# Three engines in program order in the neighbourhood attention, bias as one row of keys, weight splits last in a step

## The chip, the cores and the metric

The kernel runs on one core of a Trainium2 chip. Its engines work in parallel, each through its own list of instructions: TensorE (PE; its weight loads are PEld), VectorE (DVE), ScalarE (ACT), GpSimd (POOL), and SyncE (SP), which issues most DMAs. An instruction that needs another engine's result waits on a semaphore. The metric is the time of one execution on the device in microseconds (us).

## The reference, cut to what matters

The layer computes one input projection, two groups of attention heads, and an output projection with a residual. The change touches the second group, neighbourhood attention: 16 heads of width 64 on a grid of 16 rows x 64 columns, where each token attends to a window of 8 x 16 tokens and to 16 meta tokens.

```python
q = _rmsnorm(q, q_w); k = _rmsnorm(k, k_w)          # per head
# per grid row r: keys of 8 rows, per column a window of 16 columns
bias = rel_bias[:, dr_idx[None, :, None], dc_idx[:, None, :]]
s_win = einsum('bqhd,brqchd->bhqrc', q_row, k_win) * scale + bias
s_meta = einsum('bqhd,bmhd->bhqm', q_row, k_meta) * scale + meta_b
p = softmax(concatenate([s_win, s_meta], axis=-1), axis=-1)
o = einsum('bhqrc,brqchd->bqhd', p_win, v_win) + einsum('bhqm,bmhd->bqhd', p_meta, v_meta)
y_na = o * silu(g_na)
```

The input width is 1024, there are 1024 tokens, all in float32.

## The kernel before

Three phases follow one another. The first (to about 198 us) normalizes the input, transposes it to `hT`, and computes all gates; in its gaps it builds the relative bias (`base`, L381) and lays it out per head pair (`stage_bias`, GpSimd, written to `bias_d`). The second, which the change is about, is the neighbourhood attention, to about 735 us. Latent attention and the output projection follow.

Products in float32 are made of two halves of fewer bits: `wnh`/`wnl` of a weight, `hT`/`hTl` of the input, `qz`/`qs` of a query, two halves of keys in `kM`, of the softmax in `PT`, of values in `Vt`. The high half is a copy on ScalarE (or the other named engine), the low half a subtraction, mostly on VectorE (`lo_of`, L106), which therefore always waits for the copy.

The neighbourhood attention takes 8 head pairs of 8 tiles of 128 tokens. The loop (L691 on) runs over steps `g`. Each does a piece for four tiles at different stages: the 24 projection matmuls of the tile six ahead (`proj`, into `ps_acc`), in three parts; pv of the tile one behind (`na_pv`, `ps_o`); the transposes of the softmax of tile `g`, head 0 and head 1 (`na_ptr`, giving PT0 and PT1); the scores of the next tile (`na_qk`: TensorE into `ps_s`, VectorE adds the bias and takes the minimum into `s_sb` and `nmn`, ScalarE takes exp and its sum); the transposes of a normalized q and k (`na_tr`: on ScalarE two kM copies and two qz, then on VectorE two kM and two qs). `na_acc` takes the projection out of its bank (squares `sqn`, copy `raw`, `Vt`), every second time with the norm (`rstd`: ssn, constants, pow on GpSimd, a step of refinement). Tile 1 of a pair also projects the meta keys (16 matmuls onto `hM`). Tiles 2 to 5 load and split a quarter of the next pair's weights each. The last six steps project the latent instead (`lat_nat`).

The banks of scores and transposes are one pool of four (`bank("s")`, `bank("tr")`).

TensorE's instructions are in the order of the code. Those of ScalarE, VectorE, GpSimd and SP are ordered by the framework's scheduler when the kernel is built, by its own estimate of when each can run; on the chip every engine then follows its list.

Of the kernel before, what the change touches and what calls it, by code (L numbers as in the profile page):

```python
# [18 lines left out]
P = 128  # L19
# [15 lines left out]
WB = WI + 2 * WE  # L35
# [14 lines left out]
def hybrid_layer(ctx, tc, x, x_t, meta, meta_t, norm_w, w_na, w_g, w_lat, lat_w, w_uq, w_ukv, vec128, qpe_w, kpe_w,  # L50
# [27 lines left out]
    bias_d = dram.tile([NPAIR, P, 2, WB], F32, name="bias_d")  # L78
# [4 lines left out]

    def rstd(ss, n, cnt, np_=P, E=G):
# [3 lines left out]
        t = small.tile([P, n], F32, name="rs_t", tag=f"rs_t{n}")[:np_]  # L88
# [6 lines left out]
        G.tensor_tensor(y, v, mhalf[:np_, :n], op=ALU.pow)  # L95
        E.tensor_tensor(t, y, y, op=ALU.mult)
# [6 lines left out]
        return y  # L103

# [238 lines left out]
    base = sp1.tile([P, 16, NB, ROWS], F32, name="base")  # L343
# [33 lines left out]
    def bias_rows(rk):  # L377
        ps = bank("tr" if rk % 2 else "o")[:, :384].rearrange("p (h b) -> p h b", h=16)
        mm(ps, selr[:, rk, :], rbh, True, False)
        mm(ps, selr[:, rk, :], rbl, False, True)  # L380
        V.tensor_scalar(base[:, :, :, rk], ps, -1.0, rmask[:, rk:rk + 1], op0=ALU.mult, op1=ALU.add)  # L381


    sg = sctx.enter_context(tc.tile_pool(name="stg", bufs=1))

    imask = load(c_imask, [P, WI], "imask", sp1)
    metab = load_bc(meta_bias, 16 * NM, "metab", sp1).rearrange("p (h m) -> p h m", h=16)
    G.tensor_scalar(metab, metab, -1.0, None, op0=ALU.mult)

    def stage_bias(p):  # L390

        E = G
        bs = base[:, 2 * p:2 * p + 2].rearrange("p h b r -> p h (b r)")
        bo = sg.tile([P, 2, WB], F32, name="sgb", bufs=3)
        bi, b0, b7 = bo[:, :, :WI], bo[:, :, WI:WI + WE], bo[:, :, WI + WE:]
        mb = metab[:, 2 * p:2 * p + 2, :]
        im = imask[:, None, :].to_broadcast([P, 2, WI])
        for o, bb, w in ((0, 0, 128), (144, 8, 128), (288, 16, 112)):
            E.tensor_tensor(bi[:, :, o:o + w], bs[:, :, bb * 16:bb * 16 + w], im[:, :, o:o + w], op=ALU.add)
        E.memset(bi[:, :, 128:144], MASK)  # L400
        E.tensor_copy(bi[:, :, 272:288], mb)
        for b_, c in ((b0, 128), (b7, 0)):
            E.tensor_copy(b_[:, :, 0:128], bs[:, :, c:c + 128])
            E.tensor_copy(b_[:, :, 128:144], mb)
            E.tensor_copy(b_[:, :, 144:272], bs[:, :, c + 128:c + 256])
        G.dma_start(bias_d[p], bo)

    todo_b = list(range(NPAIR))
# [12 lines left out]
    sctx.close()  # L421
# [45 lines left out]
    def na_nat(src, n, width):  # L467

        sq = np2.tile([P, 512], F32, name="sqn")[:n, :width]
        raw = np2.tile([P, P], F32, name="natm", bufs=1)[:n, :width]  # L470
        S.activation(sq, src, AF.Square)
        S.copy(raw, src)
        return na_norm(sq, raw, n, width)

    def na_norm(sq, raw, n, width):
# [3 lines left out]
        r = rstd(ss, g, 1.0 / 64, n, V)  # L479
        r3 = raw.rearrange("p (g d) -> p g d", g=g)  # L480
        V.tensor_tensor(r3, r3, r[:, :, None].to_broadcast([n, g, 64]), op=ALU.mult)
        return raw
# [17 lines left out]
    def na_meta(p):  # L500
        d = st[p]
        acc = bank("s")
        proj(acc[:, :256], NT, d["w"], 128, 384)
        kv = np2.tile([P, 256], F32, name="kvm", bufs=1)[:NM]
        meta_sum(kv, acc[:, :256])
        Vm = VM[p % 2]
        v_split(Vm, kv[:, 128:256], NM)
        d["Vm"] = Vm
        d["natm"] = na_nat(kv[:, :128], NM, 128)
# [7 lines left out]
    def na_acc(p, t, acc):  # L517
# [43 lines left out]
    def na_qk(p, t):  # L561
# [7 lines left out]
        for j in range(2):  # L569
# [59 lines left out]
    def na_sum(p, hf):  # L629
# [9 lines left out]
               r.rearrange("p t j -> p (t j)")[:, :, None].to_broadcast([P, 8, 64]))  # L639
        ps = bank("tr")  # L640
# [20 lines left out]
    def lat_nat(t, acc, q, sq, pieces=None):  # L661
# [570 lines left out]
def _tables():  # L1232
# [30 lines left out]
    im[:, 0:128] = cm[:, 0:128]  # L1263
    im[:, 144:272] = cm[:, 128:256]
# [50 lines left out]
```

## Time and profile before

| | |
|---|---|
| median of 3 runs | 1379.38 us (1378.87 to 1380.16) |
| profiled execution | 1379.65 us, of which the span 1377.8 us |
| mean granted clock of TensorE | 0.985 |
| busy, share of the span | PE 96%, PEld 88%, DVE 70%, ACT 59%, POOL 32% |
| the chain that ended last | PE 69%, DVE 15%, ACT 4%, DMA 3% |

The profile is of one execution. A busy time is the time in which the engine ran an instruction; a timeline row gives in square brackets how long the engine had been idle before and which instruction's end let it go on. A row of groups gives after the bar the busy time, the mean length of one, and the idle time ahead of the group with its releasers.

### The profile page before, as it was taken

Reading aid. Unit: us, or ns where it says so; the run is one execution under the profiler, and the core shown is the slowest. Engines: PE = TensorE matmul, PEld = TensorE weight load, DVE = VectorE, ACT = ScalarE, POOL = GpSimd, SP = SyncE. Lnnn points to the kernel's source line nnn. Section 1 sums busy time; section 2 is a strip of 40 time slices with the busy share of each in tenths; the row PEclk is TensorE's granted clock in tenths of the full one; section 3 lists DMA queues with packets and bytes.
Section 4 is the critical chain, followed back from the end, with each engine's and each line's share of the span. In section 5 each row is a group of like instructions: output and inputs, shape, how many; then the busy total and the mean of one; then the engine's idle time right before and its main releaser. Section 6 shows DMA issues by size and latency. Waiting matters only on the chain.

```text
span 1377.8 us, 24771 instructions
## 1 busy us (share of the span) xinstructions
PE 1316.7 (96%) x8116; PEld 1214.6 (88%) x8116; DVE 958.1 (70%) x3101; ACT 809.8 (59%) x2271; POOL 436.4 (32%) x936
## 2 busy tenths in 40 slices
PE   8989998999899999999889889999999999999998
PEld 7868888998898989889889889999999999988887
DVE  4924335887877888788768998987987988642110
ACT  6522124776767777777756667777777777630110
POOL 5330472121111211132344545734734652000000
PEclk9999999999999999999999999999999999999999
DMA  9352373222322222221111100100010022254231
GB/s 342 109 175 94 125 284 91 62 78 67 98 59 78 60 74 67 74 71 55 51 43 36 55 31 21 36 28 25 27 33 29 29 77 72 83 168 130 71 109 46
DMA packets 85694, 112.24 MB, mean 81 GB/s; under 512 B 10679, under 2 KB 63287, under 8 KB 85447
## 3 DMA queue, kind: packets, MB, share of 16 engines
q1 hardware_dynamic: 84415, 102.94, 24.1%
q0 software_dynamic: 1152, 7.73, 1.4%
q8 instruction: 64, 1.05, 0.3%
q14 instruction: 63, 0.52, 0.1%
HBM read 75.12 MB, written 29.23 MB: 76 GB/s over the span
## 4 chain that ended last, share of the span: by engine, by line
PE 69%; DVE 15%; ACT 4%; DMA 3%; issue 2%; POOL 1%; SPq 0%; DVEq 0%; ACTq 0%; POOLq 0%
PE ps_acc L109 21%; PE mps_acc L109 10%; PE ps_s L109 8%; PE mps_s L109 7%; PE mps_st L109 6%; PE mps_o L109 5%; PE ps_tr L112 4%; PE mps_tr L112 4%; PE ps_o L109 4%; DVE u_na L626 2%; DVE m_sb L988 1%; DVE PT L106 1%; DVE mPT L106 1%; ACT m_sb L997 1%; DMA Vp<-Vt 1%
## 5 line engine op out<-in xcount | busy, mean ns | idle before, releaser
L95 POOL TENSOR_TENSOR rs_y<-rs_v,mhalf 128x1 f32<-128x1 f32 (+5 forms) x170 | 148.2, 875 | 139.4 <-DVE rs_v L91 115.4
L109 PE MATMUL ps_acc<-wnh,hT 128*128 128x384 f32 (+1 forms) x432 | 163.3, 378 | 6.0 <-DVE Vt L106 4.5
L109 PE MATMUL ps_acc<-wnl,hT 128*128 128x384 f32 (+1 forms) x432 | 147.2, 341 | 0.0
L109 PE MATMUL ps_acc<-wnh,hTl 128*128 128x384 f32 (+1 forms) x432 | 147.1, 340 | 0.0
L547 POOL CAST qs<-qz 64x128 fp32r<-64x128 f32 x128 | 42.1, 329 | 298.3 <-ACT qz L543 281.2
L109 PE MATMUL mps_s<-mkT,mq 128*128 128x346 f32 (+1 forms) x576 | 132.1, 338 | 1.4 <-DVE mPT L106 1.0
L578 ACT ACTIVATE s_sb<-s_sb,nmn 128x400 f32<-128x400 f32 (+1 forms) x128 | 76.9, 601 | 61.2 <-DVE nmn L576 47.8
L109 PE MATMUL mps_o<-mPT,mV 128*128 128x256 f32 x768 | 106.2, 287 | 0.0
L1014 ACT CAST mPT<-mps_tr 128x512 fp32r<-128x512 f32 x128 | 74.4, 583 | 51.1 <-PE mps_tr L112 50.2
L988 DVE TENSOR_SCALAR_CACHE_REDUCE m_sb<-mps_s 128x346 f32<-128x346 f32 (+1 forms) x192 | 97.1, 512 | 9.0 <-PE mps_s L109 7.1
L106 DVE TENSOR_TENSOR mPT<-mps_tr,mPT 128x512 fp32r<-128x512 f32 x128 | 87.6, 685 | 13.3 <-ACT mPT L1014 12.1
L109 PEld LDWEIGHTS mps_s<-mkT,mq 128*128 128x128 f32 x576 | 93.3, 192 | 3.2 <-DVE mPT L106 1.6
L109 PEld LDWEIGHTS mps_o<-mPT,mV 128*128 128x128 f32 x768 | 94.9, 189 | 0.2
L109 PEld LDWEIGHTS ps_acc<-wnh,hT 128*128 128x128 f32 x432 | 84.7, 196 | 7.4 <-DVE Vt L106 4.8
L997 ACT ACTIVATE m_sb<-m_sb,mnm 128x1040 f32<-128x1040 f32 x64 | 74.6, 1166 | 23.2 <-DVE mnm L996 16.4
L109 PEld LDWEIGHTS ps_acc<-wnl,hT 128*128 128x128 f32 x432 | 84.6, 196 | 0.0
L109 PEld LDWEIGHTS ps_acc<-wnh,hTl 128*128 128x128 f32 x432 | 83.5, 193 | 0.0
L106 DVE TENSOR_TENSOR PT<-ps_tr,PT 128x384 fp32r<-128x384 f32 (+2 forms) x160 | 72.1, 467 | 12.7 <-ACT PT L599 11.8
L599 ACT CAST PT<-ps_tr 128x384 fp32r<-128x384 f32 (+2 forms) x160 | 62.0, 411 | 28.7 <-PE ps_tr L112 27.8
L112 PE MATMUL mps_tr<-ident,m_sb 128*128 128x128 f32 x512 | 76.7, 273 | 2.0 <-DVE mq L106 1.0
L109 PE MATMUL ps_o<-PT,Vt 128*128 128x256 f32 x256 | 60.5, 299 | 15.7 <-DVE PT L106 15.6
L106 DVE TENSOR_TENSOR kM<-ps_tr,kM 64x128 fp32r<-64x128 f32 x144 | 41.6, 289 | 34.8 <-ACT qz L543 30.1
(483 smaller groups left out, 3977.7 us busy)
## 6 DMA issues: line engine op xcount, KB each, us to landing
wnf<-in_w_na_dram SPq DMA_DIRECT2D x32, 384.0 KB, 3.3
g_d<-g SPq DMA_DIRECT2D x32, 256.0 KB, 2.7
wnf<-in_w_out_dram SPq DMA_DIRECT2D x32, 256.0 KB, 2.7
bias_d<-sgb POOLq DMA_DIRECT2D x8, 944.0 KB, 4.5
wnf<-in_w_g_dram SPq DMA_DIRECT2D x19, 384.0 KB, 6.5
Vp<-Vt SPq DMA_DIRECT2D x48, 112.0 KB, 2.2
yfo<-y_d SPq DMA_DIRECT2D x24, 192.0 KB, 2.8
b<-bias_d SPq DMA_DIRECT2D x16, 272.0 KB, 3.4
```

Of the source, the lines that this page charges most:

```text
L95: G.tensor_tensor(y, v, mhalf[:np_, :n], op=ALU.pow)
L106: eng.tensor_tensor(dst, src, f(hi), op=ALU.subtract)
L109: T.matmul(o, lhsT=l, rhs=r, start=start, stop=stop, skip_group_check=True)
L112: T.transpose(out=o, in_=i, identity=ident[: i.shape[0], : i.shape[0]])
L547: G.tensor_copy(qs[h_, j], qz[l_, j])
L578: S.activation(sb, sb, AF.Exp, scale=-1.0, bias=mn, accum_out=d["sum", t // 4][:, t % 4, j:j + 1])
L599: S.copy(pt[:n, c0:c1, 0, :], ps[:n, c0:c1])
L626: V.tensor_tensor(u[a], u[a], o[a], op=ALU.add)
L988: V.tensor_scalar(st["sb", h, t][:, ks], s_ps, -SCALE, BIG, op0=ALU.mult, op1=ALU.min, accum_out=st["mx", h, t][:, b:b + 1])
L997: S.activation(sb, sb, AF.Exp, scale=-1.0, bias=nm, accum_out=st["ms", h, t // 2][:, t % 2:t % 2 + 1])
L1014: S.copy(dh, ps)
```

## The change

For the whole loop of the neighbourhood attention, the change puts ScalarE, VectorE and GpSimd under `manual_schedule`: their lists follow the code. The code of a step is rearranged. The exps of both heads come after both minima. The second half of `rstd` and the scaling (`na_acc2`) come one odd step later. The meta keys are taken out of their bank in four pieces over tiles 1, 2 and 3. The weights' splits are the last but one thing of a step. `na_sum` is in two halves. The latent tile is scaled at the beginning of the next step (`late`). The weights of the latent projection are split over tiles 2 to 4 and 7 of the last pair.

The bias is one row of 416 keys: `base` is built with its gaps for the meta keys in place, written by one DMA, and read once per pair; VectorE adds the mask of an interior tile (`bi`, 128x800) once per pair. The copies of GpSimd are gone, and the low halves of the last two groups of gate weights move from VectorE to GpSimd. The first pair's weights are loaded and split before the last gates.

```diff
-WB = WI + 2 * WE
+WB = 416
...
+    def rstd2(vy, n, np_=P, E=G):
+
+        v, y = vy
+        t = small.tile([P, n], F32, name="rs_t", tag=f"rs_t{n}")[:np_]
...
+    basek = base.rearrange("p h (g c) -> p h g c", c=144)
...
+        V.tensor_scalar(basek[:, :, :, rk:128:16], ps.rearrange("p h (g b) -> p h g b", g=3), -1.0, rmask[:, rk:rk + 1],
+                        op0=ALU.mult, op1=ALU.add)
...
+    for k in range(2):
+        V.tensor_scalar(basek[:, :, k, 128:], metab, -1.0, None, op0=ALU.mult)
...
-        gw = g_load(gr, (G, G) if gr < 4 else (V, V))
+        gw = g_load(gr)
+        if gr == 5:
+            for k in range(4):
+                na_load(0, k)
...
-                elif gr > 3 and todo_b:
-                    stage_bias(todo_b.pop(0))
-    sctx.close()
+        if gr == 3:
+            nc.sync.dma_start(bias_d.rearrange("h p n -> p h n"), base[:, :, :WB])
+            sctx.close()
...
+    imask = load(c_imask, [P, WI], "imask", np1)
+
+    def na_bias_load(p):
+        bs = st[p]["bs"] = np2.tile([P, 2, WB], F32, name="bs")
+        nc.sync.dma_start(bs, bias_d[2 * p:2 * p + 2].rearrange("h p n -> p h n"))
+        st[p].update(b0=bs[:, :, 144:], b7=bs[:, :, :WE])
 
     def na_bias(p):
-        c = 0
-        for name, w, n in (("bi", WI, 2), ("b0", WE, 1), ("b7", WE, 1)):
-            t = st[p][name] = np2.tile([P, 2, w], F32, name=name, bufs=n)
-            nc.sync.dma_start(t, bias_d[p, :, :, c:c + w])
-            c += w
+
+        bi = st[p]["bi"] = np2.tile([P, 2, WI], F32, name="bi", bufs=1)
+        V.tensor_tensor(bi, st[p]["bs"][:, :, :WI], imask[:, None, :].to_broadcast([P, 2, WI]), op=ALU.add)
...
+        if t % 2:
+            d["vy"] = na_norm1(sq, P, 512), raw
+
+    def na_acc2(p, t):
+        d = st[p]
+        vy, raw = d["vy"]
+        na_norm2(vy, raw, P, 512)
+        d["nat"][t - 1], d["nat"][t] = raw[:, :256], raw[:, 256:]
...
+            d["p", t, j] = sb, mn
+        for j in range(2):
+            sb, mn = d["p", t, j]
             S.activation(sb, sb, AF.Exp, scale=-1.0, bias=mn, accum_out=d["sum", t // 4][:, t % 4, j:j + 1])
-            d["p", t, j] = sb
...
+    def lat_nat2(t, acc, nat, r):
+        V.tensor_scalar(nat[:, :256], acc[:, :256], r[:, 0:1], None, op0=ALU.mult)
+        V.tensor_scalar(nat[:, 256:], acc[:, 256:], r[:, 1:2], None, op0=ALU.mult)
+        nats["pe", t] = nat[:, 256:]
...
+        if late is not None:
+            late.append(lambda: lat_nat2(t, acc, nat, r))
+            return
...
+    mctx = ExitStack()
+    mctx.enter_context(tc.manual_schedule(engines={mybir.EngineType.Activation, mybir.EngineType.DVE,
+                                                   mybir.EngineType.Pool}))
...
-            if 1 < t < 6 and p + 1 < NPAIR:
-                na_load(p + 1, t - 2)
-            if t == 2 and p + 1 == NPAIR:
-                wk = w_load(lambda k: w_lat[:, 2 * k:2 * k + 2, 256:576], 320, (G, V))
...
+        if late:
+            late.pop()()
+        if on(pr) and t == 2:
+            na_meta2(p)
+        if on(b - 1) and (b - 1) % 4 == 3:
+            na_sum((b - 1) // NT, (b - 1) % NT // 4)
         if on(b):
             na_pv(*divmod(b, NT))
+        if on(pr - 2) and pr % 2:
+            na_acc2(*divmod(pr - 2, NT))
...
+            na_acc(p, t, acc)
             if t == 1:
                 na_meta(p)
-            na_acc(p, t, acc)
+            if t == 2:
+                na_meta3(p)
             if t == 3:
+                na_meta4(p)
                 na_meta_tr(p)
-            if t == 7 and p + 1 < NPAIR:
-                na_bias(p + 1)
+            if 1 < t < 6:
+                k = t - 2
+                if p + 1 < NPAIR:
+                    na_load(p + 1, k)
+                    if k == 3:
+                        na_bias_load(p + 1)
+                elif k < 3:
+                    wk.append(w_split(w_lat[:, 2 * k:2 * k + 2, 256:576], 320, (V, V)))
+            if pr == NSTEP - 1:
+                wk.append(w_split(w_lat[:, 6:8, 256:576], 320, (V, V)))
         elif a < NSTEP:
-            lat_nat(t, acc, False, np2.tile([P, 512], F32, name="sqn")[:, :256])
+            lat_nat(lt, acc, False, np2.tile([P, 512], F32, name="sqn")[:, :256], late=late)
...
+        if a % NT == 7 and on(a + 1):
+            na_bias((a + 1) // NT)
         if on(b - 1) and (b - 1) % 4 == 3:
-            na_sum((b - 1) // NT, (b - 1) % NT // 4)
+            na_sum2((b - 1) // NT, (b - 1) % NT // 4)
```

On ScalarE, an interior step of the middle of the phase, before (`PT_1738` and `PT_1740` are PT0 and PT1, `qz` the queries' high half):

```order
L578 ACTIVATE s_sb,nsum<-s_sb,nmn 128x400
L599 CAST PT_1738<-ps_tr 128x3x128
L638 COPY rx<-nr 128x512
L578 ACTIVATE s_sb,nsum<-s_sb,nmn 128x400
L599 CAST PT_1740<-ps_tr 128x3x128
L578 ACTIVATE s_sb,nsum<-s_sb,nmn 128x400
L524 ACTIVATE sqn<-ps_acc 128x256
L525 COPY raw<-ps_acc 128x256
L464 CAST Vt<-ps_acc 128x2x64
L489 CAST kM<-ps_tr 64x128 x2
L543 ACTIVATE qz_1729<-ps_tr,qkw_na 64x128 x2
```

and the same engine now (`PT_1662` and `PT_1664`):

```order
L612 CAST PT_1662<-ps_tr 128x3x128
L592 ACTIVATE s_sb,nsum<-s_sb,nmn 128x400 x2
L612 CAST PT_1664<-ps_tr 128x3x128
L481 CAST kM<-ps_tr 64x128 x2
L554 ACTIVATE qz_1653<-ps_tr,qkw_na 64x128 x2
L530 ACTIVATE sqn<-ps_acc 128x256
L531 COPY raw<-ps_acc 128x256
L460 CAST Vt<-ps_acc 128x2x64
L497 COPY kvm<-ps_s 16x256
```

PT1's copy stood ahead of the second exp of its own step, and now stands behind both; the kM copies and qz follow it directly, ahead of `sqn`, `raw` and `Vt`.

On VectorE a step with a weight split, before (`ISA s_sb` is the minimum with the bias, `PT_1738` and `PT_1740` as above):

```order
L106 TENSOR_TENSOR Vt<-ps_acc,Vt 128x128
L106 TENSOR_TENSOR PT_1738<-ps_tr,PT_1738 128x3x128
L106 TENSOR_TENSOR wnl<-wnf,wnh 128x384 x2
L576 ISA s_sb,nmn<-ps_s,bi 128x400
L576 ISA nmn 128x1
L106 TENSOR_TENSOR wnl<-wnf,wnh 128x384
L576 ISA s_sb,nmn<-ps_s,bi 128x400
L576 ISA nmn 128x1
L106 TENSOR_TENSOR wnl<-wnf,wnh 128x384
L106 TENSOR_TENSOR PT_1740<-ps_tr,PT_1740 128x3x128
L478 TENSOR_REDUCE ssn<-sqn 128x8
L106 TENSOR_TENSOR Vt<-ps_acc,Vt 128x128
```

and a step now (`PT_1661` is PT0, `PT_1663` PT1):

```order
L639 TENSOR_TENSOR u_na<-u_na,ps_o 64x512 x2
L640 TENSOR_TENSOR y_na<-u_na 128x256
L114 TENSOR_TENSOR PT_1661<-ps_tr,PT_1661 128x3x128
L587 ISA s_sb,nmn<-ps_s,bi 128x400
L587 ISA nmn 128x1
L587 ISA s_sb,nmn<-ps_s,bi 128x400
L587 ISA nmn 128x1
L114 TENSOR_TENSOR PT_1663<-ps_tr,PT_1663 128x3x128
L114 TENSOR_TENSOR kM<-ps_tr,kM 64x128 x2
L557 SCALAR_TENSOR_TENSOR qs<-ps_tr,qkw_na,qz_1652 64x128 x2
L114 TENSOR_TENSOR Vt<-ps_acc,Vt 128x128
```

The low halves of weights stood between the minima and PT1; now PT1 follows the second minimum directly, kM, qs and Vt follow PT1, and the weights follow these.

On SP, at the end of the gates, before (`wnf` are weights of the pairs, `g_d` a gate's result, `naw` the norm's weights):

```order
L258 DMA g_d<-g_1584 128x512
L143 DMA wnf<-in_w_na_dram 128x768
L258 DMA g_d<-g_1655 128x512
L143 DMA wnf<-in_w_na_dram 128x768 x2
L258 DMA g_d<-g_1698 128x512
L143 DMA wnf<-in_w_na_dram 128x768 x2
L69 DMA naw<-in_na_w_dram 128x2
L458 DMA bi<-bias_d 128x2x400
```

and now:

```order
L151 DMA wnf<-in_w_na_dram 128x768 x3
L266 DMA g_d<-g_1517 128x512
L151 DMA wnf<-in_w_na_dram 128x768
L266 DMA g_d<-g_1607 128x512
L266 DMA g_d<-g_1637 128x512
L69 DMA naw<-in_na_w_dram 128x2
L69 DMA imask<-in_c_imask_dram 128x400
L566 DMA Vp<-Vt 112x256
L565 DMA Vp<-Vm_1657 16x256 x2
L151 DMA wnf<-in_w_na_dram 128x768
```

Two loads of weights that stood ahead of `naw` are behind it now.

## Rows read from the trace of the kernel before

**Rows 1.** Stretches by engine: us, busy time and (instructions) of each, PEclk (1.00 full), DMA
```profile
150.00:197.70 47.70, 47.70 (x210) 39.08 (x209) 16.80 (x27) 9.91 (x20) 37.97 (x93) 1.00 0.62 220
317.25:563.20 245.95, 231.79 (x1445) 221.27 (x1445) 202.06 (x609) 180.67 (x536) 50.21 (x84) 0.97 0.25 72
```

**Rows 2.** Timeline from 450.5 us: start, us, engine, line, operation, out<-in, count [idle before]
```profile
450.94 0.35 PE L109 MATMUL ps_s<-kM,qz 128*128 128x400 f32 x1
...
452.59 0.57 DVE L576 CUSTOM_DVE_ANT_0 s_sb<-ps_s,bi 128x400 f32<-128x400 f32 x1
...
453.15 0.56 DVE L576 CUSTOM_DVE_ANT_0 s_sb<-ps_s,bi 128x400 f32<-128x400 f32 x1
...
453.88 0.62 ACT L578 ACTIVATE s_sb<-s_sb,nmn 128x400 f32<-128x400 f32 x1
...
457.46 0.34 PE L109 MATMUL ps_s<-kM,qz 128*128 128x400 f32 x1
```

**Rows 3.** Timeline from 443 us, all engines
```profile
444.89 0.56 DVE L106 TENSOR_TENSOR PT<-ps_tr,PT 128x384 fp32r<-128x384 f32 x1 [0.72 <-ACT PT L599]
...
445.82 0.36 PE L109 MATMUL ps_s<-wnh,hM 128*48 128x256 f32 x1
...
446.57 0.54 ACT L489 CAST kM<-ps_tr 64x128 fp32r<-64x128 f32 x2
...
447.14 0.75 ACT L543 ACTIVATE qz<-ps_tr,qkw_na 64x128 fp32r<-64x128 f32 x2
...
447.78 0.34 PE L109 MATMUL ps_acc<-wnh,hT 128*128 128x384 f32 x1
...
447.92 0.61 DVE L106 TENSOR_TENSOR kM<-ps_tr,kM 64x128 fp32r<-64x128 f32 x2 [0.66 <-ACT qz L543]
```

**Rows 4.** TensorE's waits, 232.9 to 673.9 us: total, times, longest
```profile
PE ps_o L109 <- DVE PT L106: 14.1, 12, 2.1
```

**Rows 5.** Timeline of TensorE from 498.5 us
```profile
499.08 0.39 PE L109 MATMUL ps_o<-PT,Vt 128*128 128x256 f32 x1 [2.10 <-DVE PT L106]
...
503.06 0.52 PE L109 MATMUL ps_acc<-wnh,hTl 128*128 128x384 f32 x1
503.38 0.38 PE L109 MATMUL ps_acc<-wnh,hT 128*128 128x384 f32 x1
```

**Rows 6.** VectorE's groups, four periods: busy us, mean ns | idle before, releasers
```profile
L106 DVE TENSOR_TENSOR PT<-ps_tr,PT 128x384 fp32r<-128x384 f32 x48 | 26.4, 550 | 5.8 <-ACT PT L599 5.5
...
L106 DVE TENSOR_TENSOR kM<-ps_tr,kM 64x128 fp32r<-64x128 f32 x72 | 20.8, 289 | 16.0 <-ACT qz L543 13.4 <-PE ps_acc L109 1.3
...
L478 DVE TENSOR_REDUCE ssn<-sqn 128x8 f32<-128x512 f32 x16 | 11.0, 686 | 11.1 <-ACT sqn L524 11.1
```

**Rows 7.** ScalarE's groups in the same stretch
```profile
L599 ACT CAST PT<-ps_tr 128x384 fp32r<-128x384 f32 x48 | 22.9, 476 | 13.5 <-PE ps_tr L112 13.2
```

**Rows 8.** GpSimd's groups, 150 to 198 us
```profile
L399 POOL TENSOR_TENSOR sgb<-base,imask 128x256 f32<-128x256 f32 (+1 forms) x24 | 17.5, 754 | 52.4 <-DVE base L381 51.6 <-DMA bias_d<-sgb 0.7
```

**Rows 9.** Chain of waits, 205 to 213 us: start, us, what
```profile
208.13 0.33 SPq L143
...
208.51 3.38 DMA naw<-in_na_w_dram
```

**Rows 10.** Timeline of TensorE from 207.5 us
```profile
212.46 0.69 PE L109 MATMUL ps_acc<-wnh,hT 128*128 128x384 f32 x1 [4.51 <-DVE Vt L106]
```

**Rows 11.** Timeline of GpSimd from 713 us, rstd of a latent tile
```profile
713.87 0.19 POOL L93 TENSOR_TENSOR rs_v<-ssl,cnt 128x2 f32<-128x2 f32 x1 [2.98 <-ACT sqn L673]
...
716.59 0.20 POOL L102 TENSOR_TENSOR rs_y<-rs_y,rs_t 128x2 f32<-128x2 f32 x1
```

**Rows 12.** Timeline of TensorE from 255.5 us
```profile
255.65 0.38 PE L109 MATMUL ps_o<-PT,Vt 128*128 128x256 f32 x1 [1.47 <-DVE PT L106]
...
257.69 0.33 PE L109 MATMUL ps_acc<-wnl,hT 128*128 128x384 f32 x1
257.86 0.34 PE L109 MATMUL ps_acc<-wnh,hTl 128*128 128x384 f32 x1
```

More of the change, by code (lines that the diff above doesn't have):

```diff
@@ L77, in hybrid_layer @@
     tabq_d = dram.tile([P, NT, 4, 32], F32, name="tabq_d")
-    bias_d = dram.tile([NPAIR, P, 2, WB], F32, name="bias_d")
+    bias_d = dram.tile([16, P, WB], F32, name="bias_d")
     g_d = dram.tile([16, P, D], F32, name="g_d")
@@ L82, in hybrid_layer, with rstd1 @@
     small = ctx.enter_context(tc.tile_pool(name="small", bufs=5))
-    def rstd(ss, n, cnt, np_=P, E=G):
+    def rstd1(ss, n, cnt, np_=P, E=G):
         v = small.tile([P, n], F32, name="rs_v", tag=f"rs_v{n}")[:np_]
         y = small.tile([P, n], F32, name="rs_y", tag=f"rs_y{n}")[:np_]
-        t = small.tile([P, n], F32, name="rs_t", tag=f"rs_t{n}")[:np_]
         if isinstance(cnt, float):
@@ L103, in rstd @@
         return y
+    def rstd(ss, n, cnt, np_=P, E=G):
+        return rstd2(rstd1(ss, n, cnt, np_, E), n, np_, E)
     def lo_of(dst, src, hi, eng=V):
@@ L342, in hybrid_layer @@
     lo_of(rbl, rb, rbh)
-    base = sp1.tile([P, 16, NB, ROWS], F32, name="base")
+    base = sp1.tile([P, 16, 432], F32, name="base")
+    basek = base.rearrange("p h (g c) -> p h g c", c=144)
     def rope_tab(dst, wb, cs, n, nt):
@@ L380, in bias_rows, with na_load @@
         mm(ps, selr[:, rk, :], rbl, False, True)
-        V.tensor_scalar(base[:, :, :, rk], ps, -1.0, rmask[:, rk:rk + 1], op0=ALU.mult, op1=ALU.add)
-    sg = sctx.enter_context(tc.tile_pool(name="stg", bufs=1))
-    imask = load(c_imask, [P, WI], "imask", sp1)
+        V.tensor_scalar(basek[:, :, :, rk:128:16], ps.rearrange("p h (g b) -> p h g b", g=3), -1.0, rmask[:, rk:rk + 1],
+                        op0=ALU.mult, op1=ALU.add)
     metab = load_bc(meta_bias, 16 * NM, "metab", sp1).rearrange("p (h m) -> p h m", h=16)
[L388 to L408, printed above, removed]
+    for k in range(2):
+        V.tensor_scalar(basek[:, :, k, 128:], metab, -1.0, None, op0=ALU.mult)
+    st = {}
+    def na_load(p, k):
+        if k == 0:
+            st[p] = {"w": []}
+        d = st[p]
+        d["w"].append(w_split(w_na[p, :, 2 * k:2 * k + 2, :], 384, (V, V), parts=True, own=wx if k == 3 else None))
+        if k == 3:
+            d["w"] = w_views(d["w"])
     for gr in range(2, 6):
-        gw = g_load(gr, (G, G) if gr < 4 else (V, V))
+        gw = g_load(gr)
+        if gr == 5:
+            for k in range(4):
+                na_load(0, k)
         for b in range(min(3, 16 - 3 * gr)):
@@ L465, in v_split, with na_norm1 @@
         lo_of(dst[:n, 1:3, :], s2, dst[:n, 0:4:3, :])
[L467 to L475, printed above, removed]
+    def na_norm1(sq, n, width):
         g = width // 64
@@ L478, in na_norm, with na_norm2 @@
         V.tensor_reduce(ss, sq.rearrange("p (g d) -> p g d", g=g), axis=AX.X, op=ALU.add)
-        r = rstd(ss, g, 1.0 / 64, n, V)
+        return rstd1(ss, g, 1.0 / 64, n, V)
+    def na_norm2(vy, raw, n, width):
+        g = width // 64
+        r = rstd2(vy, g, n, V)
         r3 = raw.rearrange("p (g d) -> p g d", g=g)
         V.tensor_tensor(r3, r3, r[:, :, None].to_broadcast([n, g, 64]), op=ALU.mult)
-        return raw
     def k_split(d, ps, slot, mid=None):
@@ L501, in na_meta, with na_meta2, na_meta3, na_meta4 @@
         d = st[p]
[L502 to L509, printed above, removed]
+        acc = d["am"] = bank("s")[:, :256]
+        proj(acc, NT, d["w"], 128, 384)
+        kv = d["kvm"] = np2.tile([P, 256], F32, name="kvm", bufs=1)[:NM]
+        S.copy(kv, acc[32:MW])
+    def na_meta2(p):
+        d = st[p]
+        V.tensor_tensor(d["kvm"], d["am"][:NM], d["kvm"], op=ALU.add)
+    def na_meta3(p):
+        d = st[p]
+        kv = d["kvm"]
+        d["Vm"] = VM[p % 2]
+        v_split(d["Vm"], kv[:, 128:256], NM)
+        sq = np2.tile([P, 512], F32, name="sqn")[:NM, :P]
+        S.activation(sq, kv[:, :P], AF.Square)
+        d["vym"] = na_norm1(sq, NM, P)
+    def na_meta4(p):
+        d = st[p]
+        na_norm2(d["vym"], d["kvm"][:, :P], NM, P)
+        d["natm"] = d["kvm"][:, :P]
     def na_meta_tr(p):
@@ L639, in na_sum, with na_sum2 @@
                r.rearrange("p t j -> p (t j)")[:, :, None].to_broadcast([P, 8, 64]))
+        d["rx"] = rx
+    def na_sum2(p, hf):
+        d = st[p]
+        rx = d["rx"]
         ps = bank("tr")
@@ L659, in hybrid_layer, with lat_nat @@
     order = [NT] + list(range(NT))
-    def lat_nat(t, acc, q, sq, pieces=None):
+    def lat_nat2(t, acc, nat, r):
+        V.tensor_scalar(nat[:, :256], acc[:, :256], r[:, 0:1], None, op0=ALU.mult)
+        V.tensor_scalar(nat[:, 256:], acc[:, 256:], r[:, 1:2], None, op0=ALU.mult)
+        nats["pe", t] = nat[:, 256:]
+        nats[False, t] = [nat[:, k_ * P:(k_ + 1) * P] for k_ in range(2)]
+    def lat_nat(t, acc, q, sq, pieces=None, late=None):
         n = P if t < NT else NM
@@ L679, in lat_nat @@
             return
+        if not q:
+            return lat_nat2(t, acc, nat, r)
         V.tensor_scalar(nat[:, :256], acc[:, :256], r[:, 0:1], None, op0=ALU.mult)
-        if not q:
-            V.tensor_scalar(nat[:, 256:], acc[:, 256:], r[:, 1:2], None, op0=ALU.mult)
-            nats["pe", t] = nat[:, 256:]
         nats[q, t] = [nat[:, k_ * P:(k_ + 1) * P] for k_ in range(2)]
@@ L687, in hybrid_layer @@
     NSTEP = NPAIR * NT
-    for k in range(4):
-        na_load(0, k)
+    na_bias_load(0)
     na_bias(0)
+    wk = []
+    late = []
+    mctx = ExitStack()
+    mctx.enter_context(tc.manual_schedule(engines={mybir.EngineType.Activation, mybir.EngineType.DVE,
+                                                   mybir.EngineType.Pool}))
     for g in range(-LEAD, NSTEP + 4):
@@ L705, in hybrid_layer @@
         elif a < NSTEP:
-            t = order[pr - NSTEP]
+            if pr == NSTEP:
+                wk = w_views(wk)
+            lt = order[pr - NSTEP]
             acc = bank("acc")[:, :320]
-            part = lambda c0, c1: proj(acc, t, wk, 0, 320, c0, c1)
+            part = lambda c0, c1: proj(acc, lt, wk, 0, 320, c0, c1)
         part(0, 1)
+        if late:
[4 more added lines that the diff above has]
+            na_sum((b - 1) // NT, (b - 1) % NT // 4)
         if on(b):
             na_pv(*divmod(b, NT))
+        if on(pr - 2) and pr % 2:
+            na_acc2(*divmod(pr - 2, NT))
         if on(a):
@@ L737, in hybrid_layer @@
             na_vp(*divmod(a + 1, NT))
+    mctx.close()
     nx.close()
@@ L1263, in _tables @@
     im[:, 0:128] = cm[:, 0:128]
+    im[:, 128:144] = MASK
     im[:, 144:272] = cm[:, 128:256]
```

20 lines of the change are left out of this document (6 added, 14 removed).

## The prediction

> **What bounds the kernel now.** I began with the stretches by engine. In four periods of the neighbourhood attention (a period is the eight steps of one head pair) TensorE is busy 231.79 of 245.95 us and VectorE 202.06: 61.49 us a period, 57.9 of TensorE, 50.5 of VectorE, 45.2 of ScalarE [rows 1]. TensorE bounds this phase, with VectorE 11 us behind it. In the gate phase before it TensorE does not pause (47.70 of 47.70 us [rows 1]); from about 735 us on, the code is the same in both kernels.
>
> Next, how fast TensorE could go. An interior step without a stall runs from 450.94 to 457.46, 6.52 us [rows 2]; eight of them and the 16 matmuls of the meta keys (445.82 to 447.78, 1.96 us [rows 3]) make 54.1 us. The missing 7.4 us are idle time before its matmuls (the longest by far in the waits is pv's on DVE PT, 14.1 us over 441 [rows 4]) and a lower clock after the worst of these waits: after the 2.10 us at 499.08 the matmuls at 503.06 and 503.38 still start 0.32 us apart, where 0.17 is usual (257.69 and 257.86 [rows 5, 12]). So what TensorE waits for is VectorE, although that is idle 18% of the time: it is late by what stands ahead of the wanted instruction.
>
> Then I asked what VectorE's idle time is. By groups it is kM waiting for ScalarE's qz (13.4 of 16.0 us in four periods), ssn for sqn (11.1), PT for PT's copy (5.5) [rows 6]. These are chains between ScalarE and VectorE, and the change rewrites how they are interleaved.
>
> **The change part by part.** The base is the profiled run of 1379.65 us (span 1377.8, 1.85 us outside), 0.27 us over the median of 1379.38.
>
> *Program order on three engines.* TensorE keeps its order; each of ScalarE and VectorE now does a step as the code is written. I walk one interior step by row durations. On VectorE the two mins come, and the next instruction is PT1's low half. It needs ScalarE's PT1 copy, and that now stands behind both exps, which each need a min. With the spacing of a pair that ran undisturbed, the first min starts at 452.59, and the second exp at 453.88 and ends at 454.50 [rows 2]; a PT copy of 0.476 us [rows 7] and 0.03 us to the next engine put the low half at 455.01. The second min, from 453.15, ended at 453.71 [rows 2]. VectorE stands for 1.30 us. In the kernel before, ScalarE often placed PT1's copy between the exps, and the same gap was 0.72 us (idle before 444.89 [rows 3]), or was filled with other work. The two edge tiles of a pair have shorter pieces on both sides; I count them alike. Eight steps: 10.4 us.
>
> The second gap lies behind it. kM's low half comes next on VectorE, and waits for kM's two copies and two qz on ScalarE (0.54 and 0.75 [rows 3]), which stand behind that same PT1 copy. From 1.29 us goes PT1's low half, 0.55 [rows 6], running beside them: 0.74 us. The trace has this gap in some steps (0.66 at 447.92 [rows 3]), 4.0 us in a period [rows 6]; now every step has it: 5.9 us.
>
> What remains are short dependent pieces: ssn and its constant, the reciprocal of pow in three instructions, the last weight halves behind their ScalarE copies, the meta keys, which cross four engines. Of VectorE's 11 us idle, 5.5 are the kinds above (kM 4.0, PT 1.45), so 5.5 are of this sort [rows 6]. The later second half of rstd and the split meta step take some away. Bounds 0 and 6 us; I take 3, the middle, since the parts taken out (pow's wait, one of the meta crossings) are about half.
>
> VectorE's work itself is 50.5 plus one bias add per pair. The 128x800 add is not in the trace; a subtraction of 128x384 takes 0.550 [rows 6], in proportion 1.15 us, at least 0.55; I take 1.0, nearer to the proportion since the pieces are larger. A period on VectorE is then 50.5 + 1.0 + 10.4 + 5.9 + 3.0 = 70.8, say 71 us. That is above TensorE's 54.1 and above today's 61.49: VectorE becomes the engine that never catches up, and TensorE waits about 2 us in each step. Queued behind its two waits are VectorE's kM, qs and Vt and behind these the next step's u, PT0 and mins; for PT waits pv, for kM the scores. The five score and transpose banks of a step rotate through four, so TensorE cannot run ahead past it.
>
> The first projection for a pair that uses step 0 to the last full step covers 58 steps, 7.25 periods: 7.25 x (71 - 61.49) = +69 us. With 6 us instead of 3 it is +91, with 0 it is +47; without the second gap as well +4.
>
> [...] The trace has both gaps empty where they occur, 0.72 us before PT at 444.89 and 0.66 before kM at 447.92 [rows 3].
>
> *Weight split last in the step.* The 8 low halves per pair are the same work. They now stand behind kM, qs and Vt, instead of between mins and PT as before, so they no longer fill the first gap; that is already in the 10.4.
>
> *Bias.* GpSimd's layout copies and eight writes go: GpSimd is busy 37.97 us between 150 and 197.7, at a time when TensorE does not pause [rows 1]. Nothing is gained there. The lower weight halves that move to GpSimd (8 of 128x384, 8 of 128x128) cost by the nearest row, 0.754 for 128x256 [rows 8], about 12 us, within the time freed. If this cover failed, the gates would wait by at most those 12. The reads, three per pair, become one; they are issued a step or more ahead, cost nothing now, and should cost nothing after.
>
> *The start.* Today TensorE stands 4.51 us at 212.46, for VectorE, which waits for a small load, naw, that runs from 208.51 for 3.38 us, behind weights of pair 1 that SP issues at 208.13 [rows 9, 10]. Then the clock is low again, for some 2 us more, as after the wait of [rows 5]. In the new order of SP naw stands right behind the last gate's store and ahead of those weights. I credit 6.5 us; bounds 0 and 6.7.
>
> *The end.* In the six last steps the latent projection is scaled late: VectorE's two scalings open the next step, and wait for GpSimd's chain, 713.87 to 716.79, 2.9 us [rows 11], with u, PT0 and the mins behind them. Six times 2.9 is 17; nothing if TensorE's stalls hide it.  I take 8, near the middle.
>
> Sum: 1379.65 + 69 - 6.5 + 8 = 1450 us.
>
> **The rivals.** *TensorE stays the bound and loses its stalls.* The early PT0 copy and the weights at the end could be just what pv waited for [rows 4]. For it: only 7.4 us separate a period from 54.1, and all of that is lateness, not work. Against it: the walk, in which VectorE has no room. It gives 7.25 x (54.1 - 61.49) = -54, with the start and no loss at the end 1320; half of it, 1346. Chance 0.06.
>
> *Only the first gap appears.* If ScalarE reaches kM and qz early enough, P is 50.5 + 1.0 + 10.4 = 61.9 to 64 us: 1379.65 + 3 - 6.5 + 8 = 1384, to 1399. For it: in the trace the second gap is there in a part of the steps only. Against it: ScalarE cannot start kM before PT1's copy. Chance 0.08.
>
> *The clock falls with the waits.* This is the slower side at its worst: TensorE pauses 2 us in every step. [...] From 0.17 to 0.32 us a matmul, 4 us at the low level lose 1.9 us. It decides from where a step at the low clock (6.52 x 0.32/0.17 = 12 us) outlasts VectorE's 71/8 = 8.9, so that TensorE's recovery adds to the wait instead of running inside it. If half the steps pay 1.9, P is 78: 1379.65 + 120 - 6.5 + 8 = 1501. Chance 0.14. [...]
>
> **How the numbers follow.** The walk has 0.72, its own range 1420 to 1480 (P from 67 to 75). For 8 in 10 I leave out the first rival, most of the second and the upper half of the third: 1395 to 1495. What can be told from no change is 0.2%, 2.8 us. Faster takes the first rival and a little of the second, 0.07; the same 0.03; slower 0.90.
>
> **What would show it.** VectorE's idle time of a period rises from 11 to some 20 us; PT's low half waits about 1.3 us on ScalarE's PT, 64 times, and kM's 0.7 on qz; TensorE's idle time rises above 10 us a period, with PT and kM as releasers, and the meta matmuls come 71 us apart. The stall of 4.51 us at the start is gone. It is wrong if VectorE's gap before PT stays under 0.5 us, since then ScalarE's exps run earlier than I walk them; and if the periods come at 55 us, VectorE's order never was what counted.

## The result, and the profile after

The changed kernel takes 1497.32 us (median of 4 runs, 1496.57 to 1497.51) against 1379.77 of the kernel before in the same series: a ratio of 1.085, 95% interval 1.0831 to 1.0869. That is 118 us slower, where 70 were forecast; the sign and the two gaps of the walk were right, the size was not, and the time lies 2 us outside the range.

First the stretch by engine, four periods from the meta matmuls of one pair to those of the fourth after it, in the columns of [rows 1]:

```profile
332.64:633.17 300.53, 242.18 (x1447) 231.40 (x1446) 211.04 (x612) 178.66 (x534) 50.52 (x84) 0.91 0.17 52
```

A period takes 75.1 us (300.53/4) instead of 61.49, VectorE works 52.8 and stands 22.4 us; it stood 11. TensorE waits 14.6 us a period, at a granted clock of 0.91. Next what VectorE waits for, in total us, times, and the longest, in the same stretch:

```profile
DVE PT L114 <- ACT PT L612: 41.6, 32, 1.4
DVE kM L114 <- ACT qz L554: 27.5, 32, 1.7
DVE s_sb L587 <- PE ps_s L117: 4.4, 4, 1.1
DVE u_na L639 <- ACT u_na L638: 4.2, 4, 1.0
DVE kM L114 <- ACT kM L481: 3.8, 4, 0.9
```

The first two rows are the two gaps of the walk, each in all 32 steps: 10.4 us a period before PT's low half (10.4 was forecast) and 6.9 before kM's (5.9). One step of VectorE's timeline shows them close to the lengths forecast, 1.33 us for 1.30 and 0.65 for 0.74:

```profile
492.13 0.08 DVE L587 DVE_READ_ACCUMULATOR2_ANT nmn<- 128x1 f32 x1
493.54 0.56 DVE L114 TENSOR_TENSOR PT<-ps_tr,PT 128x384 fp32r<-128x384 f32 x1 [1.33 <-ACT PT L612]
494.75 0.61 DVE L114 TENSOR_TENSOR kM<-ps_tr,kM 64x128 fp32r<-64x128 f32 x2 [0.65 <-ACT qz L554]
495.39 0.72 DVE L557 SCALAR_TENSOR_TENSOR qs<-ps_tr,qkw_na,qz 64x128 fp32r<-64x128 f32 x2
```

The next view, TensorE's waits from 232 to 800 us, holds what the prediction doesn't have:

```profile
PE ps_tr L120 <- DVE kvm L474: 43.2, 7, 6.2
PE ps_o L117 <- DVE PT L114: 41.9, 33, 1.8
PE ps_tr L120 <- DVE PT L114: 27.2, 11, 3.2
```

Seven times TensorE stands about 6 us for `kvm`, the normalized meta keys, which it transposes. Its timeline behind one of them, and VectorE's in the same microseconds:

```profile
506.36 0.28 PE L120 MATMUL ps_tr<-ident,kvm 16*128 16x16 f32 x1 [6.17 <-DVE kvm L474]
...
507.81 0.52 PE L117 MATMUL ps_acc<-wnl,hT 128*128 128x384 f32 x1
508.13 0.52 PE L117 MATMUL ps_acc<-wnh,hTl 128*128 128x384 f32 x1
```
```profile
507.25 0.59 DVE L114 TENSOR_TENSOR kM<-ps_tr,kM 64x128 fp32r<-64x128 f32 x2 [0.94 <-ACT kM L481]
...
509.94 1.40 DVE L639 TENSOR_TENSOR u_na<-u_na,ps_o 64x512 f32<-64x512 f32 x2 [1.04 <-ACT u_na L638]
```

The transpose stands at the end of TensorE's step for tile 3. VectorE comes to the keys only behind the whole of its list for that step, so TensorE must wait out its lead, and after the wait its matmuls start 0.32 us apart, as in [rows 5]. What it then delivers late, ScalarE copies late, and VectorE waits 0.94 and 1.04 us for the copies.

Finally where the phase begins and ends (shortest, middle and longest ns, first and last start in us):

```profile
L117 PE MATMUL ps_s<-wnh,hM x48: 276/279/362, 199.9 to 709.5; 128*48 128x256 f32 x48
...
L117 PE MATMUL ps_acc<-wnh,hM x8: 309/309/391, 766.6 to 771.1; 128*48 128x320 f32 x8
```

In the kernel before these are 206.0 to 629.4 and 670.9. So the meta keys of the first pair come 6 us earlier, the latent projection 95.7 us later, and from there to the end of the span it is 728.9 us instead of 706.9, another 22.

### The profile page after: what moved, and what is told of

Read it like the earlier page. It is cut to its first block, busy times and chain, and to the rows that moved or that the text cites. A ratio compares the mean times of both kernels' runs of the same rounds, so it can differ in the third digit from the quotient of the medians.

```text
span 1495.5 us, 24560 instructions
## 1 busy us (share of the span) xinstructions
PE 1342.2 (90%) x8116; PEld 1239.8 (83%) x8116; DVE 971.0 (65%) x3100; ACT 807.5 (54%) x2263; POOL 402.1 (27%) x851
## 5 line engine op out<-in xcount | busy, mean ns | idle before, releaser
L93 POOL TENSOR_TENSOR rs_y<-rs_v,mhalf 128x1 f32<-128x1 f32 (+5 forms) x170 | 154.5, 912 | 166.7 <-DVE rs_v L89 83.4
L117 PE MATMUL ps_acc<-wnh,hT 128*128 128x384 f32 (+1 forms) x432 | 168.1, 389 | 0.0
L117 PE MATMUL ps_acc<-wnh,hTl 128*128 128x384 f32 (+1 forms) x432 | 151.5, 351 | 0.0
L117 PE MATMUL ps_acc<-wnl,hT 128*128 128x384 f32 (+1 forms) x432 | 151.5, 351 | 0.0
L558 POOL CAST qs<-qz 64x128 fp32r<-64x128 f32 x128 | 37.2, 290 | 397.1 <-ACT qz L554 218.3
L117 PE MATMUL ps_o<-PT,Vt 128*128 128x256 f32 x256 | 68.2, 321 | 44.8 <-DVE PT L114 44.8
L117 PEld LDWEIGHTS ps_o<-PT,Vt 128*128 128x128 f32 x256 | 50.2, 212 | 52.2 <-DVE PT L114 52.2
L117 PEld LDWEIGHTS ps_acc<-wnh,hT 128*128 128x128 f32 x432 | 87.7, 203 | 1.0
L117 PEld LDWEIGHTS ps_acc<-wnl,hT 128*128 128x128 f32 x432 | 87.8, 203 | 0.0
L114 DVE TENSOR_TENSOR kM<-ps_tr,kM 64x128 fp32r<-64x128 f32 x144 | 41.6, 289 | 70.5 <-ACT qz L554 61.0
L117 PEld LDWEIGHTS ps_acc<-wnh,hTl 128*128 128x128 f32 x432 | 86.9, 201 | 0.0
L1048 ACT ACTIVATE m_sb<-m_sb,mnm 128x1040 f32<-128x1040 f32 x64 | 74.6, 1165 | 22.4 <-DVE mnm L1047 15.7
```

The lines of the kernel that those rows point to most:

```text
L114: eng.tensor_tensor(dst, src, f(hi), op=ALU.subtract)
L117: T.matmul(o, lhsT=l, rhs=r, start=start, stop=stop, skip_group_check=True)
L558: G.tensor_copy(qs[h_, j], qz[l_, j])
L1048: S.activation(sb, sb, AF.Exp, scale=-1.0, bias=nm, accum_out=st["ms", h, t // 2][:, t % 2:t % 2 + 1])
```

## The experiments

e1, e8 and e11 are medians of four runs each; every other experiment ran once.

**e1: the order alone.** The changed kernel without its `manual_schedule` for three engines.

```diff
-    mctx.enter_context(tc.manual_schedule(engines={mybir.EngineType.Activation, mybir.EngineType.DVE,
-                                                   mybir.EngineType.Pool}))
```

> The changed kernel, with ScalarE, VectorE and GpSimd ordered by the scheduler again; everything else of the change stays (bias row, split rstd, weight splits at the end of the code of a step, late scaling of the latent). Theory A, the order itself costs the time: VectorE's idle time falls from 22.4 us a period to about 11, the period from 75.1 to 60-63 us, the total to 1365-1395 us. Theory B, the rearranged code or the bias add costs it: the scheduler can fill little, the period stays above 70 us, the total above 1450.

It took 1367.24 us, ratio 0.9907 (0.989 to 0.9923): faster than the kernel before. Four periods of it:

```profile
310.17:556.14 245.97, 231.83 (x1447) 221.04 (x1446) 205.50 (x612) 180.09 (x532) 50.61 (x84) 0.97 0.22 63
```

61.49 us a period, as before to the hundredth, with VectorE idle 10.1. The whole loss is the order; under the scheduler the new code of a step, the splits' place and the bias add cost nothing that shows. Theory A holds. The 13 us gained lie ahead of these four periods: the first projection starts at 191.7 us instead of 197.6, and TensorE is idle for 0.1 us from 200 to 235 us, where [rows 10] has 4.51.

**e2, e3 and e5: the meta keys' wait, and the two gaps.** e2 moves the transpose of the meta keys one step later; e3 puts both exps behind PT1's copy (`na_exp` is the loop of exps, taken out of `na_qk`); e5 does both.

```diff
             if t == 3:
                 na_meta4(p)
+            if t == 4:
                 na_meta_tr(p)
```
```diff
             na_ptr(*divmod(a, NT), 1)
+        if on(a + 1):
+            na_exp(*divmod(a + 1, NT))
         part(4, 8)
```

> The changed kernel, with the transpose of the meta keys one step later (t = 4 instead of 3). Theory A: TensorE's wait of 6.2 us on kvm once a period goes, and with it the low clock behind it; VectorE's waits that follow it (0.94, 1.04, 0.8, 1.1 and 1.0 us in the period from 482.94) go too, so the period falls from 75.1 to 70-72 us, the total by 20 to 36, to 1461-1477. Theory B, VectorE bounds anyway and TensorE's wait is hidden: at most 1 us a period, 1490 or more. Theory C, TensorE's wait counts in full: 6.2 us a period, about 1450.

> The changed kernel, with both exps behind PT1's copy in the code. Theory A, VectorE's two gaps are one chain of ScalarE's work: the gap before PT1's low half (1.33 us) closes, the one before kM grows from 0.65 to about 1.5, so a step gains 0.4 to 0.5 us, a period 3.6, the total about 26: 1471. Theory B, the gaps are separate: a period gains 10.5 us, the total 76: 1421.

> The changed kernel with both edits at once, the meta keys' transpose one step later and PT1's copy ahead of the exps. Theory A, two separate losses on VectorE's list: the gains add, 75.1 - 3.35 - 3.45 = 68.3 us a period, total 1497 - 30 - 30 = 1437. Theory B, one bound under both: no more than either alone, 1460-1467.

e2 took 1466.87 us, 30 less than the changed kernel, with periods of 71.7 to 72.0; e3 took 1466.88, with 71.7; e5 1438.56, with 67.6 to 68.3. The times are those of theory A each time. In e2 the wait on `kvm` is gone. Its four periods, and what VectorE waits for in them:

```profile
323.31:610.63 287.32, 246.07 (x1447) 231.03 (x1446) 210.79 (x612) 177.66 (x533) 50.52 (x84) 0.93 0.18 54
```
```profile
DVE PT L114 <- ACT PT L612: 42.0, 32, 1.4
DVE kM L114 <- ACT qz L554: 23.4, 32, 1.4
```

VectorE works 52.7 us a period and stands 10.5 before PT, 5.9 before kM and 2.8 elsewhere; the walk had 51.5, 10.4, 5.9 and 3.0. So what the wait on `kvm` cost was not TensorE's 6.2 us but what VectorE then waited in turn, 3.3 us a period: about 1 us each before kM for qz (6.9 to 5.9), for ScalarE's copies of kM and for those of `u_na`, whose rows are gone, and 0.3 for scores. In e3 VectorE's waits over four periods are

```profile
DVE kM L114 <- ACT qz L554: 60.9, 32, 2.6
...
DVE PT L114 <- ACT PT L615: 0.7, 3, 0.2
```

The gap before PT closes (41.6 to 0.7), and four fifths of it open again before kM (27.5 to 60.9): both are one chain on ScalarE, exp, exp, PT1, kM, qz, of which e3 takes only PT1's copy off the way. So the theory had e3's time right and its gain half: the two gaps shrink by 1.9 us a period, and the rest of the 3.4 is waits for scores, 1.1 us a period in the changed kernel and not among e3's listed waits, and work of VectorE (52.2 for 52.8).

**e6 and e7: which engine's order.** VectorE alone (e6) or ScalarE alone (e7) in program order; the scheduler has the others. The edit of e6; e7 has `Activation` there:

```diff
-    mctx.enter_context(tc.manual_schedule(engines={mybir.EngineType.Activation, mybir.EngineType.DVE,
-                                                   mybir.EngineType.Pool}))
+    mctx.enter_context(tc.manual_schedule(engines={mybir.EngineType.DVE}))
```

> The changed kernel, with VectorE alone in program order; ScalarE and GpSimd ordered by the scheduler, which puts PT1's copy ahead of the exps and kM and qz between them. Theory A, VectorE's two gaps come from ScalarE's order: most of the 18 us of gaps goes, the meta keys' wait stays, 65-68 us a period, 1415-1440. Theory B, VectorE's own fixed list (nothing to put into a gap) is what costs: above 70 us a period, 1465 or more.

> The changed kernel, with ScalarE alone in program order; VectorE and GpSimd ordered by the scheduler. Theory A, ScalarE's order makes the gaps: in VectorE's list PT1 and kM still follow the minima in most steps, so the gaps stay, 68-72 us a period, 1445-1475. Theory B, VectorE's list is what costs: the scheduler fills the gaps, 60-64 us a period, 1370-1400.

e6 took 1482.75 us, periods of 75.1; e7 1406.11, periods of 64.9. That is against my theory A in both, and near theory B: VectorE's fixed list alone loses 116 us against e1, ScalarE's order alone, which I had blamed, 39. Two limits: e6 keeps TensorE's wait on `kvm` (7.6 us a period), so its loss is not the two gaps alone, and GpSimd alone in program order was not run. VectorE's longest waits in four periods of e6, and then of e7:

```profile
DVE kM L114 <- ACT qz L554: 67.6, 32, 3.8
DVE PT L114 <- ACT PT L612: 4.9, 8, 0.7
```

```profile
DVE kM L114 <- ACT qz L554: 22.2, 24, 1.5
DVE PT L114 <- ACT PT L612: 18.7, 19, 1.3
```

In e6 the gap before PT is nearly gone (1.2 us a period), and the one before kM has grown to 16.9 us a period, as in e3: ScalarE's work for a step takes its time in each of these orders, and VectorE has nothing on its list to do meanwhile. In e7 the gaps occur in 24 and 19 of 32 steps, so the scheduler fills the others with sums, norms and weights; and the wait on `kvm` is 1.2 us at most.

**e8 and e11: program order with the gaps filled.** e8 keeps the three engines in program order with e2's and e3's edits. Between PT1's low half and kM's, VectorE gets either the sums of pv (`na_u`) or the low halves of weights that were loaded a step before (`pend`); they alternate from tile to tile. The product at the end, the reciprocal and the bias add move into lighter steps. e11 gives the last ten steps back to the scheduler (the last line of the diff).

```diff
             na_ptr(*divmod(a, NT), 1)
+        if on(a + 1):
+            na_exp(*divmod(a + 1, NT))
+        if on(b):
+            na_u(*divmod(b, NT))
+        while pend:
+            pend.pop(0)()
         part(4, 8)
...
+            if t % 2 == 0:
+                k = t // 2
+                if p + 1 < NPAIR:
+                    na_load2(p + 1, k)
...
             if pr == NSTEP:
                 wk = w_views(wk)
+                mctx.close()
```

> All three engines in program order as in the changed kernel, but a step written anew: PT1's copy ahead of the exps; between PT1's low half and kM's, VectorE does the sums of pv (even tiles) or the low halves of weights loaded a step before (odd tiles); loads at tiles 0, 2, 4, 6; the meta keys' transpose a step later; the end product, the reciprocal and the bias add in lighter steps. Theory A, order as such is not bad, only gaps are: with VectorE's work of 52.8 us a period and hardly a gap, TensorE (54.1 us without stalls) bounds again, 55-60 us a period, total 1320-1355, faster than the scheduler's 1367. Theory B, two engines of nearly the same load need a scheduler: 61 us or more, 1365 or more.

> The filled order of e8 up to the last full step, the scheduler from there on. In e8 the meta keys of the last pair come 9.3 us earlier than in e1, and the loss is behind them. Theory A, the two parts add: 1367.2 - 9.3 = 1358, faster than e1. Theory B, the scheduler can't use the earlier start, because what binds at the end is VectorE's work there: 1365 or more.

e8 took 1375.24 us, ratio 0.9958 (0.9942 to 0.9975); e11 1361.57, ratio 0.9861 (0.9841 to 0.9881), the fastest of all and 6 us under e1. Four periods of e11:

```profile
306.85:546.13 239.28, 230.91 (x1446) 214.94 (x1445) 208.76 (x614) 179.98 (x533) 50.94 (x84) 1.00 0.22 65
```

A period of 59.8 us, with TensorE busy 57.7 of it at a granted clock of 1.00. The order written by hand is so 1.7 us a period better than the scheduler's, and 15.3 better than the same idea with gaps. The period is at the upper end of theory A (55 to 60): 57.7 is what TensorE is busy here, and my 54.1 was too low. e8's total missed theory A and lies where B had it: from the first latent projection, at 652.2 us in both, to the end of the span it takes 721.2 us, where e11 takes 707.6 and e1 707.2. e11 has that back, and falls 4 us short of the sum ahead of it: from the last pair's meta keys to the first latent projection it takes 46.3 us, e1 42.7.

**e4 and e9: the end.** e4 is the changed kernel with the latent tiles scaled in their own step; e9 is the changed kernel with the last ten steps by the scheduler (the last line of the diff above).

```diff
-            lat_nat(lt, acc, False, np2.tile([P, 512], F32, name="sqn")[:, :256], late=late)
+            lat_nat(lt, acc, False, np2.tile([P, 512], F32, name="sqn")[:, :256])
```

> The changed kernel, with the latent tiles of the last six steps scaled at the end of their own step, not at the beginning of the next. Theory A, the loss at the end is VectorE's gaps again (six steps of 8.8 us instead of 6.7) and what follows the loop: no gain, 1492 to 1505, since GpSimd's chain of 2.9 us now stands ahead of the same VectorE work. Theory B, the late scaling is what costs there: 12 to 14 us less, about 1484.

> The changed kernel, with the three engines given back to the scheduler from the first step that projects the latent (the last ten steps of the loop). Theory A, the 22 us that the change loses from there to the end are VectorE's and GpSimd's chains in program order (u, the reciprocal and the minima behind the late scaling): 15 to 22 us come back, 1475-1482. Theory B, they come from the later start of the latent attention, its DMAs or the clock: 1492 or more.

e4 took 1502.83 us, 5.5 more than the changed kernel: that the scaling is late helps. e9 took 1473.45, 24 less, with its periods at 75.1 as in the changed kernel. That is theory A for both, though e9 lies 1.5 us below its range. VectorE's longest waits from 764 to 830 us of the changed kernel:

```profile
DVE natl L680 <- POOL rs_y L106: 15.2, 6, 3.4
DVE PT L114 <- ACT PT L612: 8.5, 8, 1.3
```

The first is GpSimd's chain ahead of the latent scalings. Over the 64 to 70 us from about the first latent projection on, it is 17.1 us in e4, 1.4 in e9 and 1.4 in the kernel before; the second is 2.4 in e9. In e8 the first is 16.1 us and in e11 1.4, and e11 takes 13.6 us less from there on. So that chain is VectorE's longest wait there, whether the scaling is late or not, and its size fits most of the loss; that it is the only cause is not shown, since e9 and e11 change the whole order of these steps. What also goes in e9 are TensorE's waits behind 766 us in the changed kernel, on the reciprocal's broadcast `rx` and on PT:

```profile
PE ps_o L117 <- DVE PT L114: 7.8, 6, 1.8
PE ps_tr L120 <- ACT rx L651: 6.0, 1, 6.0
PE ps_tr L120 <- DVE PT L114: 4.8, 3, 2.4
```

**e10: the gates.** e1 with one line of the gate weights as it was before, the fourth quarter always in a pool of its own.

```diff
-        return w_load(lambda k: w_g[:, 2 * k:2 * k + 2, gr * 384:gr * 384 + w], w, engs, wx if gr > 2 else None)
+        return w_load(lambda k: w_g[:, 2 * k:2 * k + 2, gr * 384:gr * 384 + w], w, engs, wx)
```

> The kernel of e1 (the three engines by the scheduler) with one line of the gates as it was before: the fourth quarter of a gate weight always in its own small pool (wx), also for the first three groups. Theory A, TensorE's stalls at 76.99 and 83.81 us of the kernel before came from that pool: they return, with 5 to 6 us, 1372-1374. Theory B, they went for another reason (the order of loads): 1366-1368.

It took 1374.57 us, 7.3 more than e1 and 0.6 above the range of theory A, and TensorE's stalls are back. They were in the kernel before:

```profile
76.99 0.50 PE L109 MATMUL ps_acc<-hT,wnh 128*128 128x512 f32 x1 [1.26 <-DVE g L257]
...
83.81 0.80 PE L109 MATMUL ps_acc<-hT,wnhx 128*128 128x512 f32 x1 [2.43 <-ACT wnhx L152]
```

and in e10 they are

```profile
76.83 0.50 PE L117 MATMUL ps_acc<-hT,wnh 128*128 128x512 f32 x1 [0.78 <-DVE g L265]
...
83.60 0.51 PE L117 MATMUL ps_acc<-hT,wnhx 128*128 128x512 f32 x1 [2.38 <-ACT wnhx L160]
```

The first projection starts at 196.7 us, against 191.7 in e1 and 197.6 before. So 5 of the 6 us ahead of the phase come from this line of the change, which the list of the change leaves out and to which I had given no thought.

## Why the prediction was wrong

*The walk of a step* (chance 0.72) was right: both gaps are there, in every step, with 10.4 and 6.9 us a period for 10.4 and 5.9. VectorE's work was sized 1.3 us too low (52.8 for 51.5).

*The step that failed* is "What remains are short dependent pieces: ... the meta keys, which cross four engines", with "Bounds 0 and 6 us; I take 3". Beside the two gaps VectorE stands 5.1 us a period (22.4 - 10.4 - 6.9). With the second gap and the work that makes 75.1 instead of 71, 30 of the 47 us that the sum of 1450 lacks. The term counts those pieces as waits of VectorE only. The meta keys' transpose is an instruction in TensorE's fixed list, and the change put VectorE's part of it at the end of a step without moving it. TensorE waits 6.2 us, and that comes back to VectorE as late copies and scores. e2 gives its size, 3.3 us a period and 30 in all; whether the low clock that goes with the wait (0.50 from 503 to 509 us) adds to it was not separated. Without the wait the terms of the walk come out as forecast, except VectorE's work, and the period is 71.8.

*The end* was sized at 8 us, near the middle of 0 and 17, and measured 22, which is 14 more of the 47; the last 3 are not traced. The chain that the prediction named is there: 15.2 us of VectorE's waiting on GpSimd, near the bound and not the middle. What the prediction left out are the waits for PT in the same steps (8.5 us, 2.4 in e9). With the 30 of e2 and the 24 of e9 taken off, 1497 is 1443, and the forecast without its 8 us for the end is 1442; no run has both edits.

*The start* came out at 6 us by accident. The stall of 4.51 us at naw is gone, as forecast, but the first meta transpose put one of 4.59 in its place:

```profile
215.16 0.28 PE L120 MATMUL ps_tr<-ident,kvm 16*128 16x16 f32 x1 [4.59 <-DVE kvm L474]
```

5 of the 6 us were won in the gates (e10). There the prediction's "TensorE does not pause" was read from a row that begins at 150 us, and the stalls lie at 77 and 84. e1, which has both gains, took 13 us off.

*The rivals.* The one with the falling clock (0.14) gave 1501, near the time by luck. Its 4 us at the low clock and its half of the steps were estimates of mine, and that every second step loses 1.9 us was not shown. In the kernel before the clock was 0.50 for 3.4 us, from 500.0 to 503.4, behind the wait of 2.10 us that ended at 499.08, and 1.00 from 254 to 262 us, around the wait of 1.47 us that ended at 255.65. In the changed kernel, in the period from 482.94 us the clock falls in two steps and not in half of them: within the wait on `kvm`, and behind one of 3.23 us for PT. Two stretches in the columns of [rows 1], where 0.50 is the clock:

```profile
503.00:509.00 6.00, 2.64 (x11) 2.61 (x12) 4.56 (x15) 2.97 (x9) 2.02 (x3) 0.50 0.00 0
534.00:540.00 6.00, 5.19 (x18) 5.18 (x19) 3.82 (x13) 3.25 (x11) 0.58 (x2) 0.50 0.02 4
```

The second wait, and VectorE's wait for scores behind it:

```profile
532.12 0.41 PE L120 MATMUL ps_tr<-ident,raw 128*128 128x128 f32 x2 [3.23 <-DVE PT L114]
```
```profile
540.04 0.58 DVE L587 CUSTOM_DVE_ANT_0 s_sb<-ps_s,bi 128x400 f32<-128x400 f32 x1 [1.09 <-PE ps_s L117]
```

In e2 the mean clock of four periods is still 0.93, for 0.91, and the 30 us are back all the same; how much the low clock costs in either kernel stays open. That TensorE could gain 7.4 us a period was wrong as well: in e11, at a granted clock of 1.00, it is busy 57.7. Eight times the step from 450.94 in [rows 2] is too little, since the next step, with four transposes more, takes 7.28 us without a listed wait. And the sentence that blames ScalarE's order was too narrow, as e6 shows: with VectorE's list fixed, both orders of ScalarE that were run leave a gap, and other work in the gap helps (e7, e8).

## What to carry to other kernels

When engines that feed each other are put into program order, list for each the instruction that stands behind every wait: a low half right behind its high half was a gap here in each of 32 steps (41.6 us before PT and 27.5 before kM in four periods), and work of another tile has to be written into it. Do the same for the engine that was in order already, since its list also holds instructions whose producers have just been moved. Such a wait wasn't paid here at its own length but by what it made late on the engine that bounds (6.2 us on TensorE, 3.3 us a period).

## What was not expected of the hardware

In the changed kernel TensorE's granted clock fell from 1.00 to 0.50 twice in the period from 482.94 us. It was 0.50 from 503 to 509 us, from within the wait of 6.17 us that ended at 506.36 to some 3 us behind it, and again from 534 to 540 us, behind the wait of 3.23 us that ended at 532.12 and through one of 1.41 us that ended at 534.81. Four periods of the kernel before, each with one wait of 2.1 us, had 0.97 on average, as had those of e1; those of e11, where TensorE's longest listed wait is 0.6 us, had 1.00.
